# Mixer of a two-layer trunk: another interleaving of five lanes of work (three start and step numbers of the planner)

## The chip, the cores and the metric

The kernel runs on one core of a Trainium2 chip. The core has five engines that each follow their own instruction queue in order: PE (matrix products; PEld is its loading of stationary operands), DVE (vector), ACT (activations), POOL and SP (here only the issue of transfers). They wait for each other through semaphores. The metric is the time of one execution on the device in microseconds (us), as the median of several runs.

## The reference, cut to what matters

The trunk has two residual layers over 256 tokens of width 1024, each scaled, shifted and gated by sums of a conditioning vector ("modulation", adaLN). The change lies in layer 0's mixer, which computes

```
proj = h @ w_in                                   # 1024 -> q, k, v, z (512 each), b, a, u (512)
qkv  = silu(causal_conv(qkv, conv_w))             # q, k, v: four heads of 128
o    = gated_delta_rule(l2norm(q) * 128 ** -0.5, l2norm(k), v, g, beta)   # chunks of 64 tokens
y_a  = rmsnorm(o, gdn_norm_w) * silu(z)
y_b  = s5_glu(u, ...)                             # 32 groups of a complex diagonal recurrence, then GLU
x    = x + g1 * (concatenate([y_a, y_b]) @ w_out)
mod  = cond @ ada_w[layer] + ada_b[layer]         # sh1, sc1, g1, sh2, sc2, g2
```

The triangular solve of the delta rule is done by doubling: blocks of 2, 4, ... 32 rows are inverted one after another. Behind the mixer stand a dense SwiGLU, and layer 1 with attention and a mixture of eight experts, which the change does not touch.

## The kernel before, in words

`even_layer` first forms layer 0's shift and scale sums, normalises x and projects u. Then it hands the mixer's body to `weave` (line 510), a planner that takes lanes: each lane is a Python generator whose every `next` records one step of instructions, with a start and a step length in abstract units. `weave` always advances the lane whose clock stands lowest. Lines 484 to 487 give it five lanes:

```
w = self.WEAVE
self.weave((0, w[0], self.w_in_steps(hT)), (w[1], w[2], self.s5_steps()), (w[3], w[4], self.ahead(self.gdn_steps(0), self.HG)),
           (w[5], w[6], self.ahead(self.gdn_steps(1), self.HG)), (w[7], w[8], self.ada(0, range(8, 20))))
```

- `w_in_steps`: 12 blocks of q, k and v (two of k, two of q, two of v for the first pair of heads, then the same for the second), each 24 products on PE into `pqkv` (lines 399 to 401), a split of the weights in a high part (ACT, line 132, `whi`) and a rest (DVE, line 133, `wlo`), and a convolution of one ACT and three DVE instructions (`cacc`, line 845); then four steps of z (`pz`). Two PSUM banks serve `pqkv` and `pz` in turn, so a block waits for the convolution two blocks ahead of it.
- `s5_steps`: 16 pairs of groups. A pair is two input products on PE (`bu`, line 1105), then on DVE two products with cosine and sine tables (lines 1113, 1114), an add and a subtraction (1115, 1116), two scans (1118) and a product (1121), one product on POOL (1122); four pairs end in output products on PE (`py`, line 1131) and a DVE step into `uT` (1132). The tables of the last two blocks of four pairs are computed on the way (`s5_tables`, DVE lines 686 to 693, POOL, ACT).
- `gdn_steps(0)` and `gdn_steps(1)`: the delta rule for two heads each. It begins with sums of squares (`pss`, copied by DVE line 892), reciprocal roots on POOL, and their broadcast on PE (`prow`, line 902), used on DVE (`qkvs`, `qe`, line 904); then five doubling rounds, in which PE (`pp`, `pq`, line 935) and DVE (`PP` line 970, `XT` 977, `X` 979) take turns; then four steps of the recurrence and a norm.
- `ada`: 12 sums of layer 0's later modulation, each a weight load (SP), products on PE (`gv`, line 273; `gvb`, lines 298 and 302) and small steps on ACT, DVE or POOL.

What `weave` records is a priority: a scheduler then gives each engine its final queue, by its own estimate of when things are ready. Behind the lanes come S5's gate projection (`s5_glu`, `pglu`) and the output projection (`out_proj`, `po`), in which the parts that need the second pair of heads come last.

Of the kernel before, what the change touches and what calls it, by code (L numbers as in the profile page):

```python
# [73 lines left out]

class Trunk:
    MAG = 1.5 * 2.0 ** 23
    WEAVE = (3.14, 4, 3.8, 22, 2.79, 36, 2.57, 26, 4.91)
    CUT = 14
    SEQ = (0, 1, 2, 3, 4, 5, 6, 7, 12, 13, 14, 15, 16, 17, 18, 19, 8, 9, 10, 11, 20, 21, 22, 23)
    NPE = 1  # L80
# [330 lines left out]
    def even_layer(self, upto, ent):  # L411
# [71 lines left out]

        w = self.WEAVE
        self.weave((0, w[0], self.w_in_steps(hT)), (w[1], w[2], self.s5_steps()), (w[3], w[4], self.ahead(self.gdn_steps(0), self.HG)),
# [1361 lines left out]
```

## Time and profile before

| | |
|---|---|
| runs shown | 1394.41, 1397.74, 1400.36 us; median 1397.74 us |
| the profiled execution | 1397.9 us, its span 1395.8 us (2.1 us around it) |
| mean granted PE clock | 0.964 of full speed |
| busy over the span | PE 1280.6 us (92%), DVE 829.4 us (59%), ACT 578.0 us (41%), POOL 119.1 us (9%) |
| the mixer's lanes | about 67 to 300 us of the span |

The profile is one execution. "Busy" counts an engine's instructions; idle time is given with the instruction of another engine that ended it. Matrix products are pipelined, so that those of a block start every 0.12 us while each is listed with 0.28 us. The clock column is the mean granted share of PE's full 2.4 GHz over a stretch; PE has two levels, 1.2 and 2.4 GHz. Starts are us from the span's first instruction.

### The profile page before, as it was taken

To read this page: it belongs to the slowest core of one execution; us is meant where nothing else is said; L and a number is where in the kernel's file an instruction comes from. 1 tells how busy PE (TensorE), PEld (TensorE's weight loads), DVE (VectorE), ACT (ScalarE), POOL (GpSimd) and SP (SyncE) were. 2 spreads that over 40 slices of the span, in tenths; PEclk is the share of its full clock that TensorE was granted. 3 is DMA by queue.
4 is the path that set the end of the run, shared out by engine and by line. 5 is a ranking of instruction groups with operands and counts; after the bars stand their busy time and mean duration, and the time that the engine had idled before them with its cause. 6 is when DMAs were issued, how large, how long until landed. Compare 5 with 4: busy or idle time off the path is not lost.

```text
span 1395.8 us, 26742 instructions
## 1 busy us (share of the span) xinstructions
PE 1280.6 (92%) x10928; PEld 947.1 (68%) x10928; DVE 829.4 (59%) x1516; ACT 578.0 (41%) x990; POOL 119.1 (9%) x118
## 2 busy tenths in 40 slices
PE   3997799989999988999999998999999889999975
PEld 2875676779999977898888635787352458845334
DVE  6689955458778877965689412987111079830202
ACT  3541432346444445455688402776110157711000
POOL 3223420000000002332000000000000000000000
PEclk9898899999999998999999999999999999999999
DMA  9721434329888876650799899999999999999995
GB/s 251 242 91 61 134 109 152 110 99 360 274 274 286 290 239 197 226 190 2 290 315 395 307 392 408 406 375 366 371 408 408 406 409 406 409 401 407 408 397 219
DMA packets 196163, 400.96 MB, mean 287 GB/s; under 512 B 14797, under 2 KB 115650, under 8 KB 196034
## 3 DMA queue, kind: packets, MB, share of 16 engines
q1 hardware_dynamic: 189610, 398.00, 77.6%
q10 hardware_dynamic: 6424, 1.19, 0.5%
q8 instruction: 87, 1.43, 0.4%
q14 instruction: 42, 0.34, 0.1%
HBM read 398.11 MB, written 1.05 MB: 286 GB/s over the span
## 4 chain that ended last, share of the span: by engine, by line
PE 48%; DMA 8%; DVE 4%; issue 1%; ACT 1%; POOL 1%; ACTq 0%; DVEq 0%; POOLq 0%
PE pab L1741 9%; DMA raw<-in_odd_expert_w 7%; PE py L1792 5%; PE pab L1685 4%; PE pab L1684 4%; PE pab L1686 4%; PE py L1718 2%; PE px L1635 2%; PE py L1719 2%; PE py L1717 2%; PE pqk L399 1%; PE pqk L400 1%; DVE yf L1812 1%; PE pqk L401 1%; DVE wlo L133 1%
## 5 line engine op out<-in xcount | busy, mean ns | idle before, releaser
L132 ACT ACTIVATE whi<-raw 128x1024 fp32r<-128x1024 f32 (+2 forms) x352 | 347.1, 1001 | 281.1 <-PE pab L400 52.0
L133 DVE TENSOR_TENSOR wlo<-raw,whi 128x1024 fp32r<-128x1024 f32 (+2 forms) x352 | 400.3, 1160 | 82.7 <-ACT whi L132 79.8
L1741 PE MATMUL pab<-raw,xg 128*32 128x512 f32 (+1 forms) x1920 | 194.6, 524 | 10.7 <-DMA raw<-in_odd_expert_w 10.6
L1741 PEld LDWEIGHTS pab<-raw,xg 128*32 128x32 f32 x1920 | 58.0, 109 | 119.6 <-issue 76.5
L1761 DVE TENSOR_TENSOR hb<-hb,pab 128x256 f32<-128x256 f32 (+1 forms) x35 | 12.4, 363 | 171.6 <-ACT hb L1760 171.1
L1685 PE MATMUL pab<-wlo,xg 128*128 128x512 f32 (+1 forms) x288 | 110.7, 385 | 3.6 <-DVE wlo L133 3.5
L1686 PE MATMUL pab<-whi,xg 128*128 128x512 f32 (+1 forms) x288 | 106.2, 376 | 0.0
L399 PE MATMUL pab<-hT,whi 128*128 128x256 f32 x352 | 101.9, 290 | 0.0
L400 PE MATMUL pab<-hT,whi 128*128 128x256 f32 x352 | 100.2, 285 | 0.1
L401 PE MATMUL pab<-hT,wlo 128*128 128x256 f32 x352 | 99.9, 284 | 0.0
L1792 PE MATMUL py<-raw,hTe 128*32 128x256 f32 (+1 forms) x1760 | 82.0, 338 | 11.8 <-DMA raw<-in_odd_expert_w 8.9
L283 DVE SCALAR_TENSOR_TENSOR adas<-raw,condr,adas 128x256 f32<-128x256 f32 x175 | 86.0, 497 | 3.1
L1684 PE MATMUL pab<-whi,xg 128*128 128x512 f32 (+1 forms) x288 | 84.4, 379 | 1.8 <-ACT whi L132 1.7
L1812 DVE TENSOR_TENSOR yf<-py,gate 32x256 f32<-32x256 f32 (+1 forms) x48 | 18.0, 374 | 102.4 <-PE py L1792 101.3
L1792 PEld LDWEIGHTS py<-raw,hTe 128*32 128x32 f32 x1760 | 51.6, 110 | 39.4 <-DMA raw<-in_odd_expert_w 13.0
L1760 ACT ACTIVATE hb<-pab 128x256 f32<-128x256 f32 (+1 forms) x35 | 11.5, 339 | 156.4 <-PE pab L1741 155.7
L400 PEld LDWEIGHTS pab<-hT,whi 128*128 128x128 f32 x352 | 67.9, 193 | 0.8 <-DVE hT L389 0.5
L399 PEld LDWEIGHTS pab<-hT,whi 128*128 128x128 f32 x352 | 68.0, 193 | 0.3
L401 PEld LDWEIGHTS pab<-hT,wlo 128*128 128x128 f32 x352 | 67.8, 193 | 0.1
L1685 PEld LDWEIGHTS pab<-wlo,xg 128*128 128x128 f32 x288 | 54.4, 189 | 19.5 <-DVE wlo L133 5.5
L1686 PEld LDWEIGHTS pab<-whi,xg 128*128 128x128 f32 x288 | 54.5, 189 | 9.8
L1684 PEld LDWEIGHTS pab<-whi,xg 128*128 128x128 f32 x288 | 51.0, 189 | 11.9 <-ACT whi L132 2.2
(465 smaller groups left out, 2522.1 us busy)
## 6 DMA issues: line engine op xcount, KB each, us to landing
raw<-in_odd_expert_w SPq DMA_DIRECT2D x215, 1024.0 KB
raw<-in_ada_w SPq DMA_DIRECT2D x48, 1024.0 KB
raw<-in_odd_expert_w SPq DMA_DIRECT2D x64, 768.0 KB
raw<-in_even_ffn_w SPq DMA_DIRECT2D x33, 1024.0 KB
raw<-in_odd_w_qkv SPq DMA_DIRECT2D x12, 1024.0 KB
raw<-in_even_w_in SPq DMA_DIRECT2D x10, 1024.0 KB
raw<-in_even_w_out SPq DMA_DIRECT2D x4, 1024.0 KB
raw<-in_odd_w_out SPq DMA_DIRECT2D x4, 1024.0 KB
```

Of the source, the lines that this page charges most:

```text
L132: act = nc.scalar.activation(hs, src, AF.Copy)
L133: dve = nc.vector.tensor_tensor(l, src, hs, op=ALU.subtract)
L283: nc.vector.scalar_tensor_tensor(s, w[:, k, :], self.condr[:, k, 0:1], s, op0=ALU.mult, op1=ALU.add)
L399: nc.tensor.matmul(out, wh[:, o:o + P], hT[:, k, 0, :], start=(k == 0), stop=False)
L400: nc.tensor.matmul(out, wh[:, o:o + P], hT[:, k, 1, :], start=False, stop=False)
L401: nc.tensor.matmul(out, wl[:, o:o + P], hT[:, k, 0, :], start=False, stop=(k == kd - 1))
L1684: PE.matmul(p[:, :m], xg[:, k, 0, :], wh[:, s], start=(k == 0), stop=False)
L1685: PE.matmul(p[:, :m], xg[:, k, 0, :], wl[:, s], start=False, stop=False)
L1686: PE.matmul(p[:, :m], xg[:, k, 1, :], wh[:, s], start=False, stop=(k == KD - 1))
L1741: PE.matmul(pu[t][32 * g:32 * g + 32], xg[:, k, 32 * t:32 * t + 32], v[:, :, g * n:(g + 1) * n], start=(k == 0 and (t == 0 or n > P)), sto ...
L1792: PE.matmul(py[32 * g:32 * g + 32, t], hs[f][t], v[:, i, g * n:(g + 1) * n], start=(f == 0 and t == 0), stop=(f == NF - 1 and t == 1))
L1812: V.tensor_tensor(yf[32 * t:32 * t + 32, q * j:q * j + q], py[s, t], gate[s, cs.start + q * j:cs.start + q * j + q], op=ALU.mult)
```

## The change

Three of the nine numbers that start and pace the lanes differ: S5 starts at 14 in place of 4 and steps by 4.0 in place of 3.8, and the lane of modulation sums starts at 30 in place of 26.

```
-    WEAVE = (3.14, 4, 3.8, 22, 2.79, 36, 2.57, 26, 4.91)
+    WEAVE = (3.14, 14, 4.0, 22, 2.79, 36, 2.57, 30, 4.91)
```

Number of instructions and their operands stay as they are; queues of PE, DVE, ACT, POOL and SP are reordered from the third block of the projection to the end of the output projection. In names below, the number behind a name is the buffer's own, and differs between the two programs.

First place, PE, the third block of the projection (`pqkv`), where the first input products of S5 (`bu`) stand in it. Before:

```order
L401 MATMUL pqkv_847<-hT_456,wlo_844 128x256
L399 MATMUL pqkv_847<-hT_456,whi_843 128x256
L1105 MATMUL bu_829<-uT,wb_502 128x256
L1105 MATMUL bu_829<-uT,wb_517 128x256
L814 MATMUL pd_739<-r_99_736,cst_91 128x512
L400 MATMUL pqkv_847<-hT_456,whi_843 128x256
L401 MATMUL pqkv_847<-hT_456,wlo_844 128x256
```

and in the changed program:

```order
L399 MATMUL pqkv_833<-hT_456,whi_829 128x256
L400 MATMUL pqkv_833<-hT_456,whi_829 128x256
L401 MATMUL pqkv_833<-hT_456,wlo_830 128x256
L1105 MATMUL bu_934<-uT,wb_502 128x256
L1105 MATMUL bu_934<-uT,wb_517 128x256
L399 MATMUL pqkv_868<-hT_456,whi_864 128x256
```

The products stood 14 of the block's 24 matmuls from its end and ahead of a product of the decay tables (`pd`); now they stand behind the whole block.

Second place, DVE, where the first pair of heads' scaled queries (`qe`) stand, which need PE's broadcast `prow`. Before:

```order
L845 SCALAR_TENSOR_TENSOR cacc_1081<-pqkv_1056,colB,cacc_1081 128x255
L1113 TENSOR_TENSOR s5a_1331<-bu_1328,cos_252 128x512
L1114 TENSOR_TENSOR s5b_1332<-bu_1328,sin_253 128x512
L686 TENSOR_SCALAR tu_1433<-cst,rh 128x256 x2
L904 TENSOR_TENSOR qe_1173<-qkvs_757,prow_1180 128x512
L1115 TENSOR_TENSOR s5a_1243<-s5a_1243,s5b_1244 128x256
L1116 TENSOR_TENSOR s5a_1243<-s5a_1243,s5b_1244 128x256
```

and in the changed program:

```order
L845 SCALAR_TENSOR_TENSOR cacc_977<-pqkv_952,colB,cacc_977 128x253
L133 TENSOR_TENSOR wlo_1133<-raw_999,whi_1132 128x1024
L845 SCALAR_TENSOR_TENSOR cacc_1035<-pqkv_1010,colB,cacc_1035 128x255
L845 SCALAR_TENSOR_TENSOR cacc_1035<-pqkv_1010,colB,cacc_1035 128x254
L845 SCALAR_TENSOR_TENSOR cacc_1035<-pqkv_1010,colB,cacc_1035 128x253
L904 TENSOR_TENSOR qe_1113<-qkvs_757,prow_1120 128x512
L133 TENSOR_TENSOR wlo_1224<-raw_999,whi_1223 128x1024
L845 SCALAR_TENSOR_TENSOR cacc_1070<-pqkv_1045,colB,cacc_1070 128x255
L904 TENSOR_TENSOR qkvs_757<-qkvs_757,prow_1126 128x512
```

Before, `qe` stood among S5's steps; now it stands right behind the convolution of the seventh block and ahead of that of the eighth, with no instruction of S5 between. On PE the `prow` it reads stands behind the seventh and the eighth block in the changed program, where it stood behind the seventh alone.

Third place, PE, the last output products of S5 (`py`), the second pair of heads' last doubling rounds (`pp`, `pq`), and the first products of the gate projection (`pglu`), which need S5's end. Before, the last `py` and what follows it:

```order
L1131 MATMUL py_2188<-s5a_2177,ncT_544 32x256
L935 MATMUL pp_2206<-XT_1314,M_1271 64x64 x5
L273 MATMUL gv_2260<-raw_2257,condr 32x256 x3
L302 MATMUL gvb_2270<-cst,adas_2159 128x1 x2
L935 MATMUL pp_2217<-XT_1747,M_1706 64x64 x8
L935 MATMUL pq_2228<-PP_2215,X_1313 64x64 x8
```

and in the changed program:

```order
L1131 MATMUL py_2344<-s5a_2333,ncT_544 32x256
L935 MATMUL pq_2264<-PP_2245,X_1653 64x64 x7
L1016 MATMUL pS_2283<-vb_2233,kd_1336 128x128 x2
L1023 MATMUL pog_2235<-vb_2233,QK_1217 64x128 x2
L935 MATMUL pq_2264<-PP_2245,X_1653 64x64
L935 MATMUL pq_2264<-X_1653,PP_2245 64x64 x8
L1079 MATMUL pglu_2582<-gT_2565,whi_2578 128x256
L1079 MATMUL pglu_2599<-gT_2565,whi_2595 128x256
```

Before, 40 rows of PE's queue stood between the last `py` and the first `pglu`; now five do.

## Rows read from the trace of the kernel before

**Rows 1.** Stages: us; busy us PE, PEld, DVE, ACT, POOL; PE clock; DMA share, GB/s.

```profile
80.00:172.00 92.00, 74.18 (x518) 58.00 (x516) 87.33 (x156) 29.52 (x58) 31.21 (x26) 0.83 0.28 92
172.00:250.00 78.00, 76.55 (x892) 54.26 (x894) 41.59 (x94) 21.73 (x48) 11.70 (x10) 0.93 0.41 139
250.00:300.00 50.00, 47.01 (x366) 38.87 (x361) 23.69 (x51) 19.68 (x44) 2.67 (x4) 1.00 0.18 60
```

**Rows 2.** DVE by line, 67 to 313 us: busy us, mean ns of one | idle before.

```profile
L1118 DVE TENSOR_TENSOR_SCAN s5c<-mag,s5a 128x256 f32<-128x256 f32 x32 | 24.3, 794 | 1.1 <-PE py L1131 1.1
L845 DVE SCALAR_TENSOR_TENSOR cacc<-pqkv,colB,cacc 128x255 f32<-128x255 f32 (+2 forms) x36 | 16.6, 468 | 0.1
L1121 DVE TENSOR_TENSOR s5a<-s5c,cos 128x512 f32<-128x512 f32 x16 | 13.7, 857 | 0.0
L1113 DVE TENSOR_TENSOR s5a<-bu,cos 128x512 f32<-128x512 f32 x16 | 10.9, 678 | 3.0 <-PE bu L1105 2.7 <-ACT tn L698 0.3
L1114 DVE TENSOR_TENSOR s5b<-bu,sin 128x512 f32<-128x512 f32 x16 | 10.8, 675 | 1.4 <-POOL tu L694 1.4
L1115 DVE TENSOR_TENSOR s5a<-s5a,s5b 128x256 f32<-128x256 f32 x16 | 8.5, 532 | 0.1
L1116 DVE TENSOR_TENSOR s5a<-s5a,s5b 128x256 f32<-128x256 f32 x16 | 7.7, 480 | 0.0
...
L686 DVE TENSOR_SCALAR tu<-cst,rh 128x256 f32<-128x256 f32 x8 | 4.0, 543 | 1.0 <-ACT tn L698 1.0
```

**Rows 3.** DVE in order of time: start us, us, instruction.

```profile
79.86 0.68 DVE L1113 TENSOR_TENSOR s5a<-bu,cos 128x512 f32<-128x512 f32 x1
80.46 0.68 DVE L1114 TENSOR_TENSOR s5b<-bu,sin 128x512 f32<-128x512 f32 x1
...
83.78 1.23 DVE L133 TENSOR_TENSOR wlo<-raw,whi 128x1024 fp32r<-128x1024 f32 x1 [0.66 <-ACT whi L132]
```

**Rows 4.** PE in order of time, the first input products of S5.

```profile
77.59 1.13 PE L1105 MATMUL bu<-uT,wb 32*128 32x256 f32 x4
```

**Rows 5.** PE, a later pair, a modulation sum, a doubling step.

```profile
199.83 1.07 PE L273 MATMUL gv<-raw,condr 128*32 128x256 f32 x16
...
201.26 1.12 PE L1105 MATMUL bu<-uT,wb 32*128 32x256 f32 x4
202.32 0.70 PE L298 MATMUL gvb<-adas,cst 128*128 128x256 f32 x2
...
203.46 0.63 PE L935 MATMUL pp<-XT,M 64*64 64x64 f32 x16
```

**Rows 6.** PE in order of time: a pair's products end.

```profile
114.90 1.14 PE L1105 MATMUL bu<-uT,wb 32*128 32x256 f32 x8
```

**Rows 7.** DVE in order of time: it waited for those products.

```profile
116.06 0.69 DVE L1113 TENSOR_TENSOR s5a<-bu,cos 128x512 f32<-128x512 f32 x1 [1.26 <-PE bu L1105]
```

**Rows 8.** DVE in order of time, second pair of heads begins.

```profile
164.12 0.15 DVE L892 COPY ssq<-pss 128x8 f32<-128x8 f32 x1
```

**Rows 9.** PE in order of time, its first wait for them.

```profile
167.47 2.08 PE L902 MATMUL prow<-cst,rn 128*128 128x128 f32 x8 [4.66 <-POOL rn L159]
```

**Rows 10.** POOL in order of time, ahead of the roots that PE waited for.

```profile
163.21 2.12 POOL L688 TENSOR_TENSOR tu<-tu,tn 128x512 f32<-128x512 f32 x1 [5.34 <-DVE tn L687]
165.41 0.85 POOL L158 TENSOR_SCALAR rsq<-ssq 128x4 f32<-128x4 f32 x2
```

**Rows 11.** Products of two projection blocks alone: us, busy us (count), clock, DMA share, GB/s.

```profile
91.40:96.60 5.20, 5.02 (x24) 0.57 0.54 185
118.20:121.60 3.40, 3.14 (x24) 1.00 0.00 0
```

**Rows 12.** Stage view of one stretch of 10 us, columns as in rows 1.

```profile
190.00:200.00 10.00, 10.00 (x68) 7.14 (x71) 4.82 (x13) 0.06 (x1) 1.34 (x1) 0.66 0.32 107
```

**Rows 13.** DVE in order of time, end of S5.

```profile
230.68 0.48 DVE L1132 SCALAR_TENSOR_TENSOR uT<-uT,colB,py 128x256 f32<-128x256 f32 x1 [2.20 <-PE py L1131]
...
235.26 1.29 DVE L1068 TENSOR_TENSOR gT<-uT,gT 128x512 fp32r<-128x512 f32 x2 [1.48 <-ACT gT L1067]
```

## Prediction

> **What bounds the kernel now.** I read the stages first. From 80 to 172 us DVE works 87.33 of 92 us and PE 74.18; from 172 to 250 us PE works 76.55 of 78 and DVE 41.59; from 250 to 300 us PE works 47.01 of 50 [rows 1]. So the bound changes hands: while the projection's blocks are convolved and S5's pairs run beside them, DVE is full; once the second pair of heads is in its doubling rounds, PE is full and DVE has 36 us to spare. The reader is to see in this that DVE work taken out of the first stage and done in the second costs nothing there, while PE work carried over is paid again. Then I read DVE by line: a pair of S5 is a chain of seven DVE instructions of 0.48 to 0.86 us [rows 2], far more than a block's three convolution steps. Last I read where the second pair of heads begins: DVE copies its sums of squares at 164.12 us [rows 8], POOL makes the roots, and PE takes them up at 167.47 us after a wait of 4.66 us on POOL [rows 9]. What lies ahead of that copy in DVE's queue sets when the PE-bound stage can begin.
>
> **Work that leaves the first stage.** The orders of DVE, compared up to that copy, show the changed program with 4 fewer of line 1113 and of 1114, 3 fewer of 1115 and of 1116, 6 fewer scans (1118), one fewer of 1121 and of 1132, one split `wlo` fewer, four table steps fewer (686, 687, 693), and one convolution step (845) more. By the mean durations [rows 2] that is 2.71 + 2.70 + 1.60 + 1.44 + 4.76 + 0.86, for 1132 0.48 [rows 13], for `wlo` 1.23 [rows 3], and for the four table steps, bounded by line 686's, 2.17, less 0.47: 17.5 us. Instructions in a row overlap: two steps listed with 0.68 us start 0.60 apart [rows 3], so 26 instructions give back 26 × 0.08 = 2.1 us. The copy comes **15.4 us** earlier in DVE's work.
>
> **The roots on POOL.** Before, a table product of 2.12 us stood ahead of the roots, which began at 165.41 us [rows 10], 1.14 us after the copy's end (164.12 + 0.15) [rows 8]. In the changed queue of POOL the roots stand ahead of it: **+1.1 us**; below, nothing, if another product of S5 is under way then.
>
> **New waits, first stage.** At its first place S5's `bu` moves behind 14 of a block's 24 products and ahead of `pd`. A block is 3.14 us at the granted clock of 1.00 and 5.02 us at 0.57 [rows 11], so 14 of 24 are 1.8 to 2.9 us, less 1.13 for `pd`, which I take to last as long as `bu`. Before, `bu` started at 77.59 us [rows 4]; now at 78.3 to 79.4 or, if `pd` did not matter, up to 80.5. DVE takes a pair's products up 1.16 us after they start (114.90 to 116.06) [rows 6, 7], so at 79.5 to 81.7 in place of 79.86 us [rows 3], and the queue behind it (the convolutions, hence the banks of `pqkv`) waits. Between 0 and 1.8 us I take **-1.2 us**, nearer the slow clock, since the next block was the slow one.
>
> At the second place `qe` stands in DVE's queue with no S5 step ahead of it to fill, and PE's `prow` stands behind one more block. DVE waits for that block; behind it are the eighth block's convolutions. Its price is one block, 3.14 to 5.02 us [rows 11]; nothing, if PE is ahead by then. I take **-3.1 us**, the fast block, since without S5's products PE runs block after block there.
>
> **PE work carried over.** Up to the second pair's first `prow`, PE's queue has four pairs' `bu` fewer and one modulation sum fewer: 4 × 1.12 + 1.07 + 0.70 [rows 5] = 6.3 us. It must be done in the PE-bound stage, where only 1.45 us of 78 are idle [rows 1]: **-6.3 us**. The DVE work carried over, 15.4 us, makes 57.0 of 78 us there and is hidden by PE; if PE's filler around the doubling rounds ran out, it would cost (the slower rival).
>
> **End of S5.** In the third place five rows of PE's queue stand between the last `py` and `pglu`, where 40 stood. Before, from `uT` at 230.68 us to the first `gT` (half of the 1.29 us from 235.26) [rows 13] went 5.2 us. The five rows hold 16 small doubling products, as the 0.63 us of one `pp` row [rows 5], and four more: about 1 us. PE then waits 0 (if the step's parts come closer together) to 4.2 us. Before, 1.48 us of the 5.2 went to DVE's wait for ACT, which did other work in between; I take **-1.4 us**, a third.
>
> **Edits at nothing.** On SP two loads of projection weights stand one place earlier, ahead of modulation weights. The split before them waited 0.66 us on the high part [rows 3], so at most some tenths come back; the modulation sums are used only behind the mixer. The later start of their lane moves one of them over the border, counted above; the count of ACT's table loads is the same in both programs. Everything behind the mixer is the same queue and shifts as a whole.
>
> **Sum.** 15.4 + 1.1 - 1.2 - 3.1 - 6.3 - 1.4 = 4.5 us. The execution in the profile took 1397.9 us (a span of 1395.8 and 2.1 around it), 0.2 above the median of the runs, 1397.74: 1397.9 - 4.5 = **1393.4 us**.
>
> **The clock.** The granted clock of a block was 0.57 with S5's pairs around it and 1.00 where 24 products ran in one piece [rows 11]. Against a simple reading stands the stretch from 190 to 200 us: PE busy 10.00 of 10, granted clock 0.66 [rows 12]. Blocks in closer order could so save up to 1.9 us each or nothing; the sum takes nothing. The Trainium skill (TensorE: Matmul & The Clock Gate, Part 1, What's actually happening) says that the ratio of clock pulses let through follows how busy PE has been recently; by that, blocks that follow each other closely would run at full clock. By it the sum would be 4.5 + 1.9 = 6.4 us for one such block. This case's trace agrees at 118 us and not at 190 us.
>
> **The rivals.**
> *More than forecast.* The new waits at `bu`, `qe` and `pglu` are not paid, since the parts shift together: 15.4 + 1.1 - 6.3 = 10.2 us; and one slow block becomes a fast one, 0 to 1.9 us, 0.9 in the middle. 1397.9 - 11.1 = **1386.8 us**. For it speaks that DVE's waits for `bu` in the whole mixer are 2.7 us over 16 pairs [rows 2]; against it the rows of the second place, which have nothing to fill.
> *Slower.* S5 late meets the doubling rounds. In the changed DVE queue a burst of S5 stands between one half-round's updates and the next `PP`: two each of 1113, 1114 and 1118, one each of 1115, 1116 and 1121, 6.2 - 0.7 (nine overlaps) = 5.4 us. PE has for it a sum, two pairs' `bu` and a `pp`: 1.07 + 2.24 + 0.63 [rows 5] = 3.9 us. PE then idles 1.5 us; at ten half-rounds 15 us, less 4.5: **1408.4 us**. It decides once idle time of PE between 172 and 250 us rises by over 4.5 us from 1.45 [rows 1]. Against it: DVE has 36 us to spare in that stage [rows 1].
> *Nothing moves.* The change does less than its words: `bu` moves only by part of a block, and S5's first pair stands where it stood among DVE's convolutions. The stalls come to 10.3 in place of 5.7 us (`qe` 5.0, `bu` 1.8, `pglu` 3.5), and the gain is gone: **1397.9 us**.
>
> **How the numbers follow.** Forecast 0.45, more 0.25, slower 0.13, nothing 0.17. The bounds of the unknown costs put the forecast's own range at 1389 to 1399. What a measurement of this kernel can tell from no change is about 0.5%, 7.0 us: 1390.7 and 1404.7 are the borders. The rival with more lies below the lower one, and so does a fifth of the forecast's own range, 0.09 in all: faster 0.34, slower 0.13, same 0.53. The range of 1384.5 to 1403 leaves out the slower rival and the last few hundredths of the rival with more.
>
> **What would show it.** Right: the second pair's sums of squares are copied some 11 us earlier than 164.12 us (15.4 less the first two stalls, 4.3), DVE's busy time from 172 to 250 us rises to about 57 us, PE idles there no more than some 3 us, and `qe` shows a wait of some 3 us on PE's `prow`. Wrong: the copy moves by less than 5 us (nothing moves) or by 14 or more with no wait at `qe` (more), or PE's idle time in the stage of the doubling rounds grows by over 4.5 us, ended by DVE's `PP`, `XT` or `X` (slower).

## The result and the profile after

The changed kernel takes 1385.96 us (median of 5 runs, 1385.21 to 1390.37), the kernel before 1397.74 us: a ratio of 0.9923, with a 95% interval of 0.9898 to 0.9948 (the ratio on record is that of the mean times, 1387.07 and 1397.82 us, and not of the medians). By the medians that is 11.8 us less, where 4.5 us had been forecast. In a second set of runs (below) it was 1386.11 against 1396.17 us, a ratio of 0.9927 [0.9904, 0.9951].

The profiled execution after has a span of 1384.0 us where before had 1395.8. The last product of the output projection starts at 302.76 us; before, at 310.36. So, between these two profiles, 7.6 of the 11.8 us are gained by the end of the mixer, and 4.2 us behind it, in code that neither its order nor its operands distinguish from before.

The stages of after, with the columns of [rows 1]:

```profile
80.00:172.00 92.00, 74.40 (x545) 57.95 (x545) 78.75 (x140) 30.16 (x59) 27.69 (x23) 0.87 0.28 91
172.00:250.00 78.00, 75.19 (x918) 55.59 (x919) 53.99 (x119) 24.46 (x51) 17.89 (x13) 0.96 0.46 150
250.00:300.00 50.00, 48.12 (x359) 40.61 (x358) 24.25 (x50) 19.08 (x46) 2.67 (x4) 1.00 0.17 56
```

DVE is no longer full in the first stage (78.75 of 92 us) and works 12.4 us more in the second, which PE hides, as forecast (PE idles 2.8 of 78 us there, after 1.5). PE's busy time hardly differs in either stage; its granted clock does, 0.87 and 0.96 where 0.83 and 0.93 stood.

DVE of after in order of time, at the places that the prediction spoke of:

```profile
81.03 0.69 DVE L1113 TENSOR_TENSOR s5a<-bu,cos 128x512 f32<-128x512 f32 x1 [1.40 <-PE bu L1105]
...
115.29 1.23 DVE L133 TENSOR_TENSOR wlo<-raw,whi 128x1024 fp32r<-128x1024 f32 x1 [5.04 <-ACT whi L132]
116.43 1.51 DVE L845 SCALAR_TENSOR_TENSOR cacc<-pqkv,colB,cacc 128x255 f32<-128x255 f32 x3
118.08 0.69 DVE L904 TENSOR_TENSOR qe<-qkvs,prow 128x512 f32<-128x512 f32 x1
...
151.40 0.62 DVE L686 TENSOR_SCALAR tu<-cst,rh 128x256 f32<-128x256 f32 x2 [2.72 <-ACT tn L698]
...
156.51 0.15 DVE L892 COPY ssq<-pss 128x8 f32<-128x8 f32 x1
```

The wait at S5's first product is there (81.03 where 79.86 stood, [rows 3]). At the second place `qe` waits for nothing: the wait falls four instructions ahead of it, on the split of a later block's weights, whose high part ACT makes only when PE has read the seventh block's (PE's eighth block starts at 114.11 us, before that split is done). It is 5.04 us long. DVE had no step of S5 in its queue there, as the order shows. The copy of the second pair's sums comes at 156.51 in place of 164.12 us [rows 8].

POOL and PE behind that copy:

```profile
156.74 1.71 POOL L158 TENSOR_SCALAR rsq<-ssq 128x4 f32<-128x4 f32 x2 [2.81 <-DVE ssq L892]
158.53 1.99 POOL L159 TENSOR_TENSOR rn<-rsq,mhalf 128x4 f32<-128x4 f32 x2
```

```profile
159.59 2.08 PE L902 MATMUL prow<-cst,rn 128*128 128x128 f32 x8 [5.86 <-POOL rn L159]
```

The roots start 0.2 us behind the copy in place of 1.3 [rows 8, 10], but their first step takes 1.71 us for two in place of 0.85, so only 0.3 of the 1.1 us arrive at PE: copy to `prow` is 3.08 us after 3.35 [rows 8, 9].

**Behind the mixer.** In the profile of before the granted clock falls there at two places, in windows with the columns of [rows 1]:

```profile
570.00:580.00 10.00, 9.17 (x63) 8.41 (x60) 8.89 (x33) 7.78 (x22) 5.76 (x6) 0.86 0.66 217
620.00:630.00 10.00, 10.00 (x70) 8.82 (x69) 6.86 (x28) 5.43 (x17) 5.04 (x6) 0.92 0.33 107
630.00:640.00 10.00, 10.00 (x86) 9.44 (x85) 5.10 (x13) 5.96 (x19) 3.51 (x5) 0.91 0.00 1
```

The same work in the profile of after, 8 us earlier:

```profile
562.00:572.00 10.00, 9.18 (x74) 8.36 (x74) 8.89 (x34) 7.91 (x23) 5.75 (x6) 1.00 0.72 233
612.00:622.00 10.00, 10.00 (x77) 9.08 (x75) 6.29 (x24) 5.83 (x22) 5.66 (x6) 1.00 0.34 107
622.00:632.00 10.00, 10.00 (x86) 8.94 (x86) 6.82 (x19) 6.15 (x16) 2.72 (x4) 1.00 0.00 0
```

Whether that belongs to the change is the first question for the experiments.

### The profile page after: what moved, and what is told of

The parts are those of the page before. It is cut to its first block, busy times and chain, and to the rows that moved or that the text cites. A ratio compares the mean times of both kernels' runs of the same rounds, so it can differ in the third digit from the quotient of the medians.

```text
span 1384.0 us, 26734 instructions
## 1 busy us (share of the span) xinstructions
PE 1271.2 (92%) x10928; PEld 941.6 (68%) x10928; DVE 830.7 (60%) x1516; ACT 578.8 (42%) x990; POOL 121.1 (9%) x118
## 4 chain that ended last, share of the span: by engine, by line
PE 49%; DMA 8%; DVE 2%; issue 1%; ACT 1%; POOL 1%; SPq 1%; ACTq 0%; DVEq 0%; POOLq 0%
PE pab L1741 9%; DMA raw<-in_odd_expert_w 7%; PE py L1792 5%; PE pab L1685 5%; PE pab L1686 4%; PE pab L1684 4%; PE py L1718 2%; PE px L1635 2%; PE py L1719 2%; PE py L1717 2%; PE pqk L399 1%; PE pqk L400 1%; PE pqk L401 1%; PE pth L151 1%; PE psc L1306 1%
## 5 line engine op out<-in xcount | busy, mean ns | idle before, releaser
L1761 DVE TENSOR_TENSOR hb<-hb,pab 128x256 f32<-128x256 f32 (+1 forms) x35 | 12.4, 363 | 173.7 <-ACT hb L1760 173.2
L1792 PEld LDWEIGHTS py<-raw,hTe 128*32 128x32 f32 x1760 | 51.6, 110 | 36.3 <-DMA raw<-in_odd_expert_w 10.2
L1686 PEld LDWEIGHTS pab<-whi,xg 128*128 128x128 f32 x288 | 54.7, 190 | 10.1
```

The lines of the kernel that those rows point to most:

```text
L1686: PE.matmul(p[:, :m], xg[:, k, 1, :], wh[:, s], start=False, stop=(k == KD - 1))
L1792: PE.matmul(py[32 * g:32 * g + 32, t], hs[f][t], v[:, i, g * n:(g + 1) * n], start=(f == 0 and t == 0), stop=(f == NF - 1 and t == 1))
```

## The experiments

Each kernel was profiled once and timed in five rounds beside the kernel before. The table goes by PE, all in us: the start of the second pair's copy and of the last product of the output projection, both counted from the first product of the projection's first block ("copy", "mixer"); in that stretch PE's idle time and its busy time where the granted clock was 1.2 GHz ("low"); from that last product to the span's end ("behind"); the median of the runs, and the ratio on record to the runs of before that were timed beside them (medians 1397.74 us for after, 1396.36 for E1 to E4, 1396.17 for E5 to E8 and 1396.43 for E9 to E12), with its interval. The ratio is not the quotient of the medians. The other columns come from one execution each; runs of one kernel spread by up to 20 us (E3 from 1382.78 to 1396.31, E4 from 1378.03 to 1395.83, E10 from 1380.0 to 1400.39).

| kernel | copy | mixer | idle | low | behind | median | ratio |
|---|---|---|---|---|---|---|---|
| before | 96.6 | 242.9 | 22.5 | 33.1 | 1085.5 | 1397.74 | |
| E1 before again | 96.8 | 243.0 | 22.7 | 33.0 | 1081.7 | 1396.93 | 1.0014 [0.9999, 1.0029] |
| after (14, 4.0, 30) | 89.4 | 235.6 | 22.3 | 24.7 | 1081.3 | 1385.96 | 0.9923 [0.9898, 0.9948] |
| E5 after again | 89.6 | 236.0 | 21.9 | 26.2 | 1081.5 | 1386.11 | 0.9927 [0.9904, 0.9951] |
| E2 start alone (14, 3.8, 26) | 86.5 | 240.5 | 19.9 | 48.1 | 1081.9 | 1391.32 | 0.9960 [0.9941, 0.9980] |
| E3 lane alone (4, 3.8, 30) | 90.3 | 235.2 | 20.3 | 39.4 | 1082.5 | 1385.51 | 0.9947 [0.9924, 0.9970] |
| E4 step alone (4, 4.0, 26) | 97.7 | 229.5 | 22.0 | 19.6 | 1081.0 | 1382.95 | 0.9915 [0.9885, 0.9945] |
| E6 start and step (14, 4.0, 26) | 88.4 | 237.6 | 19.9 | 36.0 | 1084.4 | 1390.41 | 0.9961 [0.9943, 0.9979] |
| E7 start later (24, 4.0, 30) | 88.5 | 249.7 | 22.7 | 56.5 | 1081.5 | 1401.28 | 1.0038 [1.0023, 1.0053] |
| E8 step and lane (4, 4.0, 30) | 90.3 | 231.9 | 19.9 | 26.5 | 1078.4 | 1384.83 | 0.9930 [0.9903, 0.9957] |
| E9 before, apart | 96.7 | 237.0 | 22.6 | 26.2 | 1080.6 | 1388.43 | 0.9947 [0.9921, 0.9974] |
| E10 after, apart | 89.5 | 246.2 | 25.3 | 58.9 | 1082.3 | 1395.73 | 0.9968 [0.9937, 0.9999] |
| E11 step alone, apart | 97.7 | 228.8 | 21.0 | 22.9 | 1082.0 | 1378.82 | 0.9867 [0.9846, 0.9888] |
| E12 step and lane, apart | 90.2 | 232.9 | 19.2 | 32.7 | 1081.3 | 1387.54 | 0.9930 [0.9904, 0.9955] |

**E1, before again.** No edit.

> The kernel before, unchanged, for a second profile. Both theories: the second pair's sums of squares are copied at 164.1 us and the last product of the output projection starts at 310.4 us, each within 0.5 us, since the queues are the same. They differ behind that: in the profiles of before and after, the stretch from that product to the end of the span is 1085.4 and 1081.2 us with the same instructions. Theory A (the granted clock behind the mixer falls by chance, from one execution to the next): this second profile of before gives a stretch 2 us or more away from 1085.4. Theory B (the dips of the clock behind the mixer are tied to the program's own timing): 1085.4 again, within 0.7 us, with the dips near 577 and 630 us at the same place.

The mixer repeated itself within 0.1 us; the stretch behind it came out 3.7 us shorter, and the clock did not fall where it had. The same places in E1:

```profile
572.00:582.00 10.00, 9.18 (x78) 8.49 (x79) 8.89 (x33) 8.14 (x23) 5.76 (x6) 1.00 0.69 222
622.00:632.00 10.00, 10.00 (x76) 9.08 (x76) 6.00 (x22) 6.06 (x23) 5.51 (x6) 1.00 0.34 107
632.00:642.00 10.00, 10.00 (x85) 8.82 (x84) 7.08 (x19) 5.88 (x15) 2.73 (x4) 1.00 0.00 0
```

So theory A holds: those 4.2 us came from one execution of before, not from the change (E6, another order of the mixer, has 1084.4 us there and E8 1078.4). (The starts expected by the span's own clock were missed by 2.5 us, since the part ahead of the mixer was that much longer; the later tables count from the mixer's first product.)

**E2, E3, E4: one number each.** The edits:

```
E2:  WEAVE = (3.14, 14, 3.8, 22, 2.79, 36, 2.57, 26, 4.91)
E3:  WEAVE = (3.14, 4, 3.8, 22, 2.79, 36, 2.57, 30, 4.91)
E4:  WEAVE = (3.14, 4, 4.0, 22, 2.79, 36, 2.57, 26, 4.91)
```

> Only S5's start goes from 4 to 14; its step stays at 3.8 and the modulation lane's start at 26. Theory (S5's later start alone takes DVE work out of the stretch ahead of the second pair's sums of squares): that copy at 156.5 us within 1.5 us, the mixer's last product at 302.8 within 1.5 us, total 1385 to 1391 us, some 8 to 12 us below before. Rival (the modulation lane, by its weight loads and products, frees the stretch): copy at 162 to 164 us, total within 3 us of before.

> Only the modulation lane's start goes from 26 to 30; S5 keeps 4 and 3.8. Its DVE queue has, ahead of the second pair's copy, 2 fewer of lines 1113, 1114 and 1118, one split and one table step fewer: by the rows of before about 5.5 us. Theory (S5's start does it, and this lane only lets the scheduler shuffle a little): copy 0 to 5.5 us earlier than 164.1 us, the mixer's end 0 to 4 us earlier, total 1393 to 1398 us. Rival (the lane is what pays): the mixer's end at 303 us, total 1386 to 1389 us.

> Only S5's step goes from 3.8 to 4.0. Its DVE queue has one scan and one table step more ahead of the second pair's copy, 1.3 us. Theory: no gain, copy at 164 to 166 us, total within 2 us of before. Rival (the slower pace of S5 is what frees DVE): copy 3 us or more earlier, total 4 us or more below before.

E2 moves the copy even further forward than the change does (86.5 us), and its mixer is only 2.4 us shorter than before's: the last product starts at 307.3 us, 4.5 us later than expected. E3, the lane that should have done little, gives 7.7 us in its profile, as its rival had it, and more than its copy moved (6.4 us); by its runs (0.9947) it is not ahead of the change (0.9923). E4, expected to do nothing, has the copy 1 us later and a mixer 13.4 us shorter. From the copy to the mixer's end the three take 154.0, 144.9 and 131.8 us, where both before and after take 146.2. The copy does not set the end. PE's clock goes with the length in part: E2 has 48.1 us of busy time at the low clock, E4 19.6; but E3 has 39.4, more than before's 33.1, and a mixer 7.7 us shorter.

**E5, after again.** No edit.

> The changed kernel, unchanged, for a second profile. From the first product of the mixer's projection to the last of the output projection its first profile had 235.6 us (before: 242.9 and 243.0 in two profiles), and 1081.3 us behind that (before: 1085.5 and 1081.7). If the mixer repeats itself and the stretch behind it falls by chance, this profile has 235.6 within 0.5 us, and 1081 to 1086 us behind it, and over many runs the change is worth the mixer's 7.3 us: total 1387 to 1391 us where before has 1396.4. If the stretch behind it is part of what the change does, 1081.3 again, and a total 11 to 12 us below before.

The mixer repeats itself within 0.4 us. The stretch behind it was 1081.5 us, as in E1's profile of before (1081.7): nothing is gained there in profiles without the fall of the clock. The median, 10.1 us below before's, lies between the two expectations.

**E6, E7, E8: combinations and a later start.** The edits:

```
E6:  WEAVE = (3.14, 14, 4.0, 22, 2.79, 36, 2.57, 26, 4.91)
E7:  WEAVE = (3.14, 24, 4.0, 22, 2.79, 36, 2.57, 30, 4.91)
E8:  WEAVE = (3.14, 4, 4.0, 22, 2.79, 36, 2.57, 30, 4.91)
```

> S5's start 14 and step 4.0, the modulation lane left at 26: the change without its third number. Mixer lengths so far: 235.6 (all three), 240.5 (start alone), 235.2 (lane alone), 229.5 (step alone). Theory F (the second pair's copy sets the end, 146 us behind it): the DVE order ahead of the copy is nearly that of the start alone, copy 86 to 89 us behind the mixer's first product and a mixer of 232 to 236 us. Theory C (PE's idle time and its time at the low clock behind the copy set the end, and the copy does not): the mixer's length is 200 within 4 us plus PE's idle time in it plus half of its busy time at the low clock, wherever the copy stands.

> S5's start 24 in place of 14, the other two numbers as in the change: ahead of the second pair's copy DVE has 2 scans and one more step less than in the change, 2.1 us. Theory F: copy 2 us earlier than in the change (some 87 us behind the first product), mixer 233 to 234 us. Theory C: the copy is early and the mixer is not shorter for it: S5's pairs fall into the doubling rounds, PE waits there more often and runs longer at the low clock, mixer 236 us or more; the length is again 200 within 4 us plus idle time plus half the busy time at the low clock.

> S5's start left at 4, its step 4.0 and the modulation lane's start 30. Ahead of the second pair's copy DVE has the order of the lane alone. Theory F: copy 90 us behind the mixer's first product, as with the lane alone, mixer 235 to 236 us. If the gains of the step alone (13.4 us) and of the lane alone (7.7 us) are of two causes they add up, 222 us; Theory C gives no such sum: the length is 200 within 4 us plus idle time plus half the busy time at the low clock, and the low clock in the doubling rounds decides between 229 and 240 us.

Theory F falls: in E7 the copy comes 8.1 us earlier than before's and the mixer ends 6.8 us later, and E6 (237.6 us) and E8 (231.9) lie outside its bounds of 232 to 236 and 235 to 236. The waits that theory C expected in E7 did not come: PE's idle time is 22.7 us, before's 22.5. Its low time did come. Three of its low stretches, in windows with the columns of [rows 1]:

```profile
188.00:198.20 10.20, 10.20 (x51) 7.00 (x50) 3.73 (x10) 0.00 (x0) 0.00 (x0) 0.50 0.32 103
229.00:239.20 10.20, 9.16 (x107) 6.22 (x109) 9.18 (x19) 0.38 (x1) 3.81 (x3) 0.50 0.29 89
249.40:259.60 10.20, 10.20 (x88) 6.27 (x80) 2.04 (x7) 2.71 (x4) 0.00 (x0) 0.50 0.32 104
```

E8 shows that the gains of E3 and E4 do not add up (231.9, not 222 us). Theory C's rule, length less idle time less half of the low time, gives 203.8 for before, 201.0 for after, and 196.6, 195.1, 197.8, 199.8, 198.7 and 198.8 us for E2, E3, E4, E6, E7 and E8: E3 lies 0.9 us outside its bounds of 196 to 204, the others within; of the later kernels E10, with 191.4, lies 4.6 us outside. The rule is rough, since half of the low time is too much for small products, which do not take twice as long there (0.40 us from start to start at 191.40 to 192.19 us of before, where 0.26 stood), but it tells the extremes apart: E4 and E7 differ by 36.9 us of low time and 20.2 us of length. Between them it leaves up to 12.4 us that neither waits nor the clock account for, more than the change is worth.

The mean granted clock that stands on record for every run says the same without the profiles. One less this clock, times the span, is the time that the clock can have cost at most. After's second set loses 42.7 us by it and the runs of before beside it 51.6, so up to 8.9 of the 10.2 us between their mean times can be the clock's. E3's runs lose as much as those of before (52.3 and 52.0 us) and are 9.2 us shorter; E2's lose 4.5 us more and are 6.2 us shorter. So the clock alone does not order these kernels.

**What stands ahead of a fall of the clock.** Long waits of PE do (after's 5.86 us at 159.59, and 1.2 GHz from 156.9 us). But before's clock also falls at 191.5 us, where PE's row shows no idle time at all:

```profile
185.00:191.50 6.50, 6.50 (x53) 5.45 (x52) 2.73 (x3) 2.39 (x3) 0.00 (x0) 1.00 0.19 67
191.50:198.30 6.80, 6.80 (x40) 4.49 (x41) 4.45 (x12) 0.00 (x0) 0.68 (x1) 0.50 0.46 155
```

PE of before in order of time, in that stretch:

```profile
188.06 0.33 PE L935 MATMUL pq<-X,PP 64*64 64x64 f32 x2
188.32 0.33 PE L918 MATMUL pkk<-qkvs,qkvs 128*64 128x64 f32 x2
188.57 0.33 PE L935 MATMUL pq<-X,PP 64*64 64x64 f32 x2
...
191.40 0.46 PE L918 MATMUL pkk<-qkvs,qkvs 128*64 128x64 f32 x2
...
192.19 0.47 PE L918 MATMUL pkk<-qkvs,qkvs 128*64 128x64 f32 x2
```

The first pair's doubling products and the second pair's key products alternate one by one, 0.26 us each, while a piece of 8 is listed with 0.63 us in all (`pp`, [rows 5]; each product stands twice in the trace, so x16 is 8 and x2 is one). PE is listed as busy and starts about a quarter as many products. The long run of them goes from 188.06 to 192.66 us, 16 products, and the clock falls in it. After has the same pattern from 179.56 to 184.25 us, 18 products, and the same fall:

```profile
177.00:184.20 7.20, 7.20 (x60) 5.86 (x58) 2.62 (x3) 2.39 (x3) 0.00 (x0) 1.00 0.16 43
184.20:191.00 6.80, 6.80 (x26) 4.73 (x26) 5.73 (x17) 0.00 (x0) 0.00 (x0) 0.50 0.32 113
```

In E4 a block of z's products stands between two shorter runs (185.10 to 187.22 and 190.16 to 192.03 us), and the clock stays up:

```profile
183.00:187.20 4.20, 4.20 (x43) 2.97 (x39) 1.31 (x3) 0.80 (x3) 2.60 (x3) 1.00 0.69 218
187.20:190.10 2.90, 2.90 (x25) 2.83 (x24) 1.64 (x4) 2.80 (x4) 0.62 (x1) 1.00 0.14 46
190.10:192.00 1.90, 1.90 (x20) 1.37 (x21) 1.74 (x4) 1.33 (x2) 0.00 (x0) 1.00 0.00 0
192.00:199.00 7.00, 7.00 (x64) 4.13 (x64) 7.00 (x17) 0.28 (x1) 0.31 (x1) 1.00 0.44 139
```

The other traces leave it at a tendency. The clock falls in such a run of 16 or 18 products, or 0.1 us behind it, in all five profiles that have one (before, after, their second profiles, and E6 at 183.4 us). Of the runs of 4 to 9 products, three have a fall inside or right behind them (E2 at 185.8 us, E3 at 177.8, E7 at 188.0) and the others have none, among them two of after (172.29 and 174.97 us), two of E4 and two of E8. What decides there is not PE's order: by line and name, PE's 137 instructions from 165.0 to 177.8 us of E3 are those from 165.2 to 178.0 us of E8, in the same order, with a run of 9 products at the end. E3:

```profile
175.40:177.80 2.40, 2.40 (x20) 1.77 (x19) 0.52 (x2) 0.79 (x2) 1.71 (x2) 1.00 1.04 364
177.80:181.20 3.40, 3.40 (x17) 3.40 (x17) 1.04 (x3) 2.25 (x4) 1.52 (x2) 0.51 0.07 23
```

and E8, whose clock stays up:

```profile
175.60:178.00 2.40, 2.40 (x20) 1.74 (x19) 0.60 (x2) 0.71 (x2) 1.62 (x2) 1.00 1.02 357
178.00:181.40 3.40, 3.40 (x29) 3.20 (x28) 1.79 (x4) 3.02 (x5) 1.53 (x2) 1.00 0.07 24
```

The Trainium skill (TensorE: Matmul & The Clock Gate, Part 1, What's actually happening) says that the ratio of clock pulses follows how busy PE has been recently; ahead of before's fall at 191.5 us the profile lists PE as busy throughout (6.50 of 6.50 us), so the trace agrees only if listed busy time is not what the rule means.

**E9 to E12: the two kinds apart.** In before, after, E4 and E8 the first pair's doubling products are ordered behind the second pair's key products, once those have been recorded:

```
-                PE.matmul(pkk[rows, 256 + b * CH: ...
+                kk = PE.matmul(pkk[rows, 256 + b * CH: ...; self.lastkk = [kk.ins] if hp == 1 else []
...
-                    PE.matmul(out[rows, b * CH:(b + 1) * CH], ...
+                    with self.behind(self.lastkk if hp == 0 else ()): PE.matmul(out[rows, b * CH:(b + 1) * CH], ...
```

> The kernel before, with one constraint more on PE's order: the first pair's doubling products stand behind the last of the second pair's key products (pkk), so that the two no longer alternate one by one. In the profile of before 18 products of the two kinds alternate from 188.06 to 192.59 us, 0.25 us each, where 8 doubling products in one piece take 0.51 us, 0.06 each; PE counts as busy all the while, and the granted clock falls to 0.50 at 191.5 us, for 6.8 us. Theory (alternating small products are slow by themselves, and the low clock behind them comes from PE doing little in them): 3 to 5 us less for the products and 3.4 us less for the clock, the mixer 234 to 237 us in place of 242.9. Rival (any other order shuffles the low clock elsewhere, and the alternation is filled with work that must be done anyway): mixer 239 to 246 us, with a low stretch of 6.8 us somewhere else in the doubling rounds.

> The changed kernel with the same constraint. Its alternating products run from 172.3 to 176.3 and from 179.6 to 184.2 us, 33 products in 8.6 us, and the clock falls at 184.2 us for 6.8 us. Theory: 4 to 6 us less for the products, 3.4 us for the clock; mixer 226 to 229 us in place of 235.6. Rival: mixer 232 to 240 us.

> The kernel with S5's step alone changed (mixer 229.5 us) and the same constraint. Its alternation is broken by a block of z's products between 187.2 and 190.2 us, and no low clock follows it, so only the products' own time is to be had: 3 to 5 us, mixer 224 to 227 us. Rival: 227 to 235 us.

> S5's step and the modulation lane's start changed (mixer 231.9 us), with the same constraint. As with the step alone, no low clock stands directly behind its alternating products; theory: 3 to 5 us less, mixer 227 to 229 us. Rival: 229 to 238 us.

In E9 the mixer has 237.0 us, 5.9 less than before, at the upper edge of the theory's 234 to 237 and outside the rival's bounds. The clock gave what was expected (6.9 us less low time, half of it 3.4), the products 2.5 us where 3 to 5 were expected. Over all runs the clock's share is smaller: by the recorded clock E9 loses at most 49.2 us to it and the runs of before beside it 50.2, while E9's mean time is 7.8 us shorter. PE of E9 in that place, and its windows:

```profile
189.36 0.69 PE L918 MATMUL pkk<-qkvs,qkvs 128*64 128x64 f32 x16
189.97 0.68 PE L935 MATMUL pq<-PP,X 64*64 64x64 f32 x16
190.49 0.63 PE L935 MATMUL pq<-X,PP 64*64 64x64 f32 x16
```

```profile
186.50:193.00 6.50, 6.50 (x86) 5.69 (x87) 5.88 (x11) 2.40 (x3) 1.28 (x1) 1.00 0.17 58
193.00:199.80 6.80, 6.80 (x79) 5.18 (x78) 5.52 (x14) 1.58 (x5) 0.00 (x0) 1.00 0.79 254
```

Eight products of either kind take 0.5 to 0.6 us, and the clock stays at 2.4 GHz. In E10 the fall at that place is gone as well, but the clock falls later for much longer:

```profile
178.00:185.00 7.00, 7.00 (x94) 5.62 (x97) 7.00 (x16) 2.39 (x3) 0.01 (x1) 1.00 0.24 83
185.00:192.00 7.00, 6.13 (x55) 5.32 (x48) 7.00 (x14) 1.15 (x3) 3.76 (x3) 1.00 0.77 250
214.70:221.50 6.80, 6.17 (x64) 4.25 (x64) 6.51 (x17) 0.74 (x2) 3.26 (x3) 0.50 0.07 28
228.40:259.10 30.70, 29.99 (x248) 24.36 (x247) 8.47 (x26) 5.50 (x10) 0.00 (x0) 0.50 0.22 69
```

Its runs lie between 1380.0 and 1400.39 us, and the profiled one is the longest of them, with a mean granted clock of 0.954 where the two runs near 1380 us have 0.962; the long low stretch is thus probably not in all of them, but no profile of a shorter one was taken. E11 and E12 miss the theory by 2 and 4 us: their products take 1.5 us less each (length less idle and half the low time: 196.3 and 197.3 in place of 197.8 and 198.8), and 3.4 and 6.2 us more of them run at the low clock. So the constraint parts the products in all four; what the rest of the mixer makes of it lies within the rival's bounds in E11 and E12, and beyond them in E10. It is shown to pay in before alone; after is no shorter with it (0.9968 against 0.9923), and in E12 the mixer is 1.0 us longer than E8's. E11 has the shortest time of all, 1378.82 us, with an interval below that of the change; the interval of E4, the same kernel without the constraint, overlaps E11's, so what the constraint adds there is not shown.

## Why the prediction was right or wrong

The measured 1385.96 us lies in the range, near its lower end; the likeliest case, 1393.4, was 7.4 us too high, and the outcome is the one that had 0.34, faster by over 0.5%; no change, at 0.53, had been held likelier. That the time lies in the range is in part luck. Up to the second pair's copy 11.1 us had been forecast and 7.3 came (counted from the mixer's first product); behind it a loss of 6.6 us (1.1 less 6.3 and 1.4) had been forecast and none came. Two misses of opposite sign left 3 us between the forecast and the mixer's gain.

- **Work that leaves the first stage**: right. From 80 us to the copy DVE is busy 64.9 us in place of 79.4 (to 156.5 and 164.1 us), 14.6 us less; 15.4 were forecast.
- **New waits, first stage**: right in kind, too small in sum. `bu` cost 1.2 us as forecast (by the span's start; 1.5 counted from the mixer's first product). The wait at the second place came, at 5.04 us, the upper bound (5.02) and not the 3.1 us chosen, and for the split, not for `qe`: PE had waited 3.28 us for POOL's roots, and the block behind that wait ran at a granted clock of 0.71. The wait of 2.72 us for the tables was not in the sum. DVE's idle time grew by 7.0 us in place of 4.3, and the copy moved by 7.6 us, not 11.1.
- **The roots on POOL**: +1.1 us forecast, 0.3 measured.
- **PE work carried over, -6.3 us**: this is the step that failed, with the end of S5 (-1.4 us) beside it. By product time at full clock (busy time less half the low time) PE did 4.8 us less ahead of the copy, but only 1.9 us more behind it, and there 0.5 us of idle and 2.8 us of low time fell away. Copy to end stayed at 146.2 us. The prediction took PE's busy time in that stage as work that must be done at its listed length. E4, E2 and E7 take 132, 154 and 161 us there, and the whole mixer, with the same instructions in all, took 229.5 to 249.7 us. At S5's end `pglu` follows `uT` by 2.3 us, and PE's five rows cover that.
- **The clock**: the sum took nothing for it. In the mixer PE's low time fell by 8.4 us from before to after (6.8 in the second profiles), and idle time hardly at all. Half of it, 4.2 of the 7.3 us (3.4 of 7.0), is an estimate of the clock's part, and a high one, since small products lose less than half. In time, the two low stretches of 3.4 us at 150.5 and 239.2 us of before have no counterpart in after, and the first one, from 89.1 us, lasts 6.8 us where after's, from 88.6, lasts 3.4; the second profiles repeat all three. Nearly all the rest, 2.8 us, is product time at the same clock. From start to start, without waits and with low time halved, `gv` and `py` together take 28.2 us in place of 29.9 and `bu` 13.9 in place of 15.1, while `pkk` takes 5.9 in place of 4.7. That their neighbours in PE's queue make the difference was not tried kind by kind, but for `pkk` (E9). The rival with more had the size (1386.8 us), though its reason, waits that are not paid, is not what happened.
- **The slower rival** did not occur here. E7, with S5 later still, is slower, its mixer 6.8 us longer than before's, but not for the rival's reason: behind the copy PE idles 7.9 us there, 8.3 in before, and has 40.6 us of low time, 13.7 in before.

What stays open: no run isolates what made after's mixer shorter; each of the three numbers alone gave another mixture of low time and product time. The medians differ by 10.1 to 11.8 us, the mixers by 7.0 to 7.3. The part ahead of the mixer, the same code in all kernels, varies by 4.8 us between the profiles, and with its low time: 65.6 us with 10.2 us of it, 69.7 to 70.4 with 23.9. The part behind varies by 7 (1078.4 to 1085.5). So the remaining 3 to 4.5 us may be chance or not. Why the low stretches of the mixer come at the same places in both profiles of before, and of after, and why E10's runs spread over 20 us, was not tried either.

## What to carry to other kernels

In the stage that PE bounded here, listed busy time was no measure of work: look at start-to-start times of small products, and at the granted clock in the windows behind them, before pricing work that is moved into such a stage. Price a fall of the clock as a chance, since one order of PE met it in one kernel and not in another (E3, E8). A change of order was not a sum of moved durations: settings one number away from before (E2, E3, E4) gave mixers of 240.5, 235.2 and 229.5 us, and the one that brought the copy forward furthest gained least. Repeat the profile of the kernel before, and subtract stretches that the change cannot touch, before explaining a difference; one profile of a kernel whose runs spread by 10 us or more is one draw.

## What the runs showed that was not expected

Products of 64 and of 128 rows that alternate one by one start 0.26 us apart, where either kind in a piece starts 0.06 to 0.08 us apart; and the clock fell to 1.2 GHz in such runs, with PE listed as busy throughout (before at 191.5, after at 184.2 us), and not at that place where they were apart (E9). It did not fall behind every such run: the same order of PE fell in E3 and not in E8. Two profiles of one program agree within 0.1 us (before) and 0.4 us (after) over the 240 us of the mixer, and differ by 3.7 us (before) and 0.2 us (after) in the 1080 us behind it.
